# Masked softmax: batch 0 loaded as two contiguous megabytes from two queues

## The chip, the cores and the metric

One core of one Trainium2 chip. The metric is the device time of one execution in microseconds, as the median of several runs. A *span* is the length of the one execution that was profiled; it is some 1.6 us shorter than that execution's device time. A *packet* is one record of the trace's DMA table: one unbroken run of memory (8 or 16 KiB in most transfers) for SyncE and ScalarE, several short ones for GpSimd. The table doesn't name the DMA engine, so packets "per engine" are a count divided by 16.

## The reference

```python
batch, heads, seq_q, seq_k = 16, 8, 256, 256        # x: float32, 33.5 MB
for b in range(batch):
    length = lengths[b]                              # 128 <= length < 256
    masked = x[b, :, :, :length]
    masked = masked - np.max(masked, axis=-1, keepdims=True)
    e = np.exp(masked)
    result[b, :, :, :length] = e / np.sum(e, axis=-1, keepdims=True)   # the rest is 0
```

## The kernel before

A batch is 2048 rows of 256 columns, 2 MB. Partition p holds rows 16p to 16p + 15, which are 16 KiB in one piece of memory. There are eight slots of one batch each. SyncE issues the loads of batches 0 to 3 and all stores; GpSimd issues the loads of batches 4 to 15 and fetches only as many columns as the batch's length needs. VectorE clips the columns past the length to a huge negative number, ScalarE takes exponentials and row sums, and VectorE divides. A "half" is 8 of a partition's 16 rows.

```python
x_f   = x.rearrange("b h q k -> b (h q) k").rearrange("b (p t) k -> b p t k", p=P)
...
nc.scalar.dma_start(out=word64, in_=lengths[None, :]).then_inc(s_word, 16)
for h in range(2):                                   # batch 0 in two halves
    s = slice(h * half, (h + 1) * half)
    nc.sync.dma_start(out=xt[:, 0, s], in_=x_f[0, :, s]).then_inc(s_ld[h], 16)
for b in range(1, ahead):                            # batches 1, 2, 3 whole
    nc.sync.dma_start(out=xt[:, b], in_=x_f[b]).then_inc(s_ld[b + 1], 16)

nc.sync.wait_ge(s_exp, 3)                            # three half batches of exponentials
for b in range(batch):
    for s in parts(b):                               # batch 0 whole, later ones in halves or quarters
        nc.sync.wait_ge(s_out, 2 * b + (s.stop - 1) // half + 1)     # that part is divided
        ...
        nc.sync.dma_start(out=out_f[b, :, s, :], in_=xt[:, b % slots, s, :]).then_inc(...)
...
# GpSimd: waits for batch 2's landing, then two loads are under way at any time
nc.gpsimd.wait_ge(s_ld[ahead - 1], 16)
with nc.Fori(0, (batch - ahead) // 2, 1, engines=[POOL]) as q:
    for par in range(2):
        ...                                          # waits for load n-2 and store n-8
        pick(v_len, ...)                             # load of batch n, w of 256 columns
...
# VectorE's order
mask(0, slice(0, half)); mask(0, slice(half, nt))    # each waits for its half
for b in range(batch):
    ...                                              # divide(0, 0), mask(1), divide(0, 1), mask(2), ...
```

The softmax here doesn't subtract the row's maximum and nothing guards it: scores larger than these inputs give would overflow.

## Time and profile before

| | before |
|---|---|
| device time | 156.19 us, median of 3 (155.84 to 156.23) |
| moved | 62.08 MB at a mean of 401 GB/s |
| VectorE, ScalarE busy | 75%, 68% |
| clips of the two halves of batch 0 start | 6.60, 9.05 us |
| first store issued | 19.86 us |
| GpSimd's first load (batch 4) issued | 20.85 us |

The lines behind this table are shown in the prediction. The queues are named as the profile names them: q1 is SyncE's, q10 ScalarE's, q0 GpSimd's.

### The profile page before, as it was taken

Reading aid. Unit: us, or ns where it says so; the run is one execution under the profiler, and the core shown is the slowest. Engines: PE = TensorE matmul, PEld = TensorE weight load, DVE = VectorE, ACT = ScalarE, POOL = GpSimd, SP = SyncE. Lnnn points to the kernel's source line nnn. Section 1 sums busy time; section 2 is a strip of 40 time slices with the busy share of each in tenths; the row PEclk is TensorE's granted clock in tenths of the full one; section 3 lists DMA queues with packets and bytes.
Section 4 is the critical chain, followed back from the end, with each engine's and each line's share of the span. In section 5 each row is a group of like instructions: output and inputs, shape, how many; then the busy total and the mean of one; then the engine's idle time right before and its main releaser. Section 6 shows DMA issues by size and latency. Waiting matters only on the chain.

```text
span 154.7 us, 1324 instructions
## 1 busy us (share of the span) xinstructions
PE 0.2 (0%) x1; PEld 0.1 (0%) x1; DVE 115.7 (75%) x84; ACT 105.2 (68%) x514; POOL 19.0 (12%) x25
## 2 busy tenths in 40 slices
PE   0000000000000000000000000000000000000000
PEld 0000000000000000000000000000000000000000
DVE  1249999952999696979979696969689629796700
ACT  3087799992692959778695959595976906959200
POOL 4910031000220110201111020202001000000000
DMA  4999999999999999999999999999999999999992
GB/s 116 426 449 424 428 398 406 398 407 447 400 410 395 402 409 414 415 417 411 404 424 407 417 408 409 415 416 416 416 417 419 419 448 415 426 445 419 430 421 85
DMA packets 9988, 62.08 MB, mean 401 GB/s; under 512 B 850, under 2 KB 946, under 8 KB 6274
## 3 DMA queue, kind: packets, MB, share of 16 engines
q1 hardware_dynamic: 5904, 41.95, 65.8%
q0 software_dynamic: 4080, 20.12, 32.1%
q14 instruction: 2, 0.02, 0.0%
q10 hardware_dynamic: 2, 0.00, 0.0%
HBM read 28.51 MB, written 33.55 MB: 401 GB/s over the span
## 4 chain that ended last, share of the span: by engine, by line
DMA 55%; DVE 19%; ACT 8%; issue 8%; ACTq 2%; SPq 1%; POOLq 1%; DVEq 0%
DMA xt<-in_x_dram 34%; DMA out_dram<-xt 21%; DVE xt L222 9%; DVE xt L195 9%; ACT xt L252 8%; ACTq L252 2%; DVE inv_sum L219 1%; SPq L109 1%; POOLq L99 0%; SPq L111 0%; SPq L120 0%; DVEq L212 0%; POOLq L135 0%; POOLq L130 0%; ACTq L247 0%
## 5 line engine op out<-in xcount | busy, mean ns | idle before, releaser
L252 ACT ACTIVATE xt<-xt x256 | 102.4, 401 | 37.2 <-DVE xt L195 37.2
L222 DVE TENSOR_TENSOR xt<-xt,inv_sum 128x2048 f32<-128x2048 f32 x32 | 73.4, 2292 | 1.1
L252 ACT ACTIVATION_READ_ACCUMULATOR xt<-xt x256 | 47.9, 187 | 0.0
L195 DVE SCALAR_TENSOR_TENSOR xt<-down,len_s,xt 128x2048 f32<-128x2048 f32 (+1 forms) x17 | 37.8, 2222 | 13.1 <-DMA xt<-in_x_dram 13.0
L130 POOL DMA_DIRECT2D xt<-in_x_dram x12 | 12.8, 1064 | 95.5 <-issue 50.6
L219 DVE RECIPROCAL inv_sum<-row_sum 128x8 f32<-128x8 f32 x32 | 6.3, 198 | 14.4 <-ACT xt L252 14.4
L149 POOL MEMSET xt<- 128x1536 f32 x4 | 5.3, 1386 | 1.1 <-DVE len_s L186 1.1
L244 ACT ACT_TABLE_LOAD x1 | 1.3, 1283 | 1.6 <-SPq L81 1.6
L178 DVE TENSOR_SCALAR down<-iota_i 128x256 f32<-128x256 int32 x1 | 0.3, 297 | 1.6 <-POOL iota_i L141 1.6
L183 DVE CAST len_b<-word 1x16 bf16<-1x16 int32 x1 | 0.2, 163 | 0.4 <-DMA word<-in_lengths_dram 0.4
L186 DVE TENSOR_SCALAR len_s<-len_f 128x16 f32<-128x16 f32 x1 | 0.2, 174 | 0.3 <-PE len_f L165 0.3
L141 POOL IOTA iota_i<- 128x256 int32 x1 | 0.3, 331 | 0.6 <-SPq L81 0.6
L146 POOL MEMSET seed<- 1x1 f32 x2 | 0.3, 162 | 0.0
L244 ACT ACTIVATE warm<-const-float32-0.0 128x1 f32<-128x1 f32 x1 | 0.2, 203 | 0.0
L144 POOL MEMSET ones<- 1x128 bf16 x1 | 0.2, 194 | 0.0
L165 PE MATMUL len_f<-len_b,ones 1*128 1x16 bf16 x1 | 0.2, 164 | 2.6 <-DVE len_b L183 2.6
L275 POOL MEMSET const-float32-0.0<- 128x1 f32 x1 | 0.1, 98 | 0.3 <-issue 0.3
L165 PEld LDWEIGHTS len_f<-len_b,ones 1*128 1x128 bf16 x1 | 0.1, 99 | 2.6 <-POOL ones L144 2.6
L275 POOL MEMSET const-float32-1.0<- 128x1 f32 x1 | 0.1, 98 | 0.0
L275 POOL MEMSET const-bfloat16-1.0<- 128x1 bf16 x1 | 0.1, 98 | 0.0
L275 POOL MEMSET const-uint8-127<- 128x1 uint8 x1 | 0.1, 98 | 0.0
L275 POOL BASE_LOAD x1 | 0.0, 17 | 0.1
## 6 DMA issues: line engine op xcount, KB each, us to landing
out_dram<-xt SPq DMA_DIRECT2D x19, 1024.0 KB
out_dram<-xt SPq DMA_DIRECT2D x14, 512.0 KB
xt<-in_x_dram SPq DMA_DIRECT2D x3, 2048.0 KB, 16.1
out_dram<-xt SPq DMA_DIRECT2D x3, 2048.0 KB
xt<-in_x_dram POOLq DMA_DIRECT2D x3, 1728.0 KB, 16.9
xt<-in_x_dram POOLq DMA_DIRECT2D x2, 2048.0 KB, 18.5
xt<-in_x_dram POOLq DMA_DIRECT2D x2, 1600.0 KB, 16.8
xt<-in_x_dram POOLq DMA_DIRECT2D x2, 1280.0 KB, 14.8
```

Source lines behind the costliest of these rows:

```text
L109: nc.sync.dma_start(out=xt[:, 0, s], in_=x_f[0, :, s]).then_inc(s_ld[h], 16)
L130: nc.gpsimd.dma_start(out=xt[:, slot, :, :w], in_=x_n[:, n, :, :w]).then_inc(s_sw[par], 16)
L141: nc.gpsimd.iota(iota_i, pattern=[[1, seq_k]], base=0, channel_multiplier=0).then_inc(s_iota, 1)
L146: nc.gpsimd.memset(seed[:, par : par + 1], 0.0).then_inc(s_st[par], 64)
L149: nc.gpsimd.memset(xt[:, b, :, low:], 0.0).then_inc(s_fill, 1)
L165: nc.tensor.matmul(len_f, lhsT=ones, rhs=len_b, start=True, stop=True).then_inc(s_lenf, 1)
L195: return nc.vector.scalar_tensor_tensor(out=t, in0=down[:, None, lo:hi].to_broadcast([P, s.stop - s.start, hi - lo]), scalar=len_s[:, b : ...
L219: step(nc.vector.reciprocal(out=inv_sum[:, b, s], in_=row_sum[:, b, s]))
L222: nc.vector.tensor_tensor(out=t, in0=t, in1=inv_sum[:, b, s, None].to_broadcast([P, half, seq_k]), op=ALU.mult,).then_inc(s_out, 1)
L244: nc.scalar.activation(out=warm, in_=nc.const_aps.tensor(0.0, (P, 1), F32), func=EXP)
L252: ins = nc.scalar.activation(out=e, in_=e, func=EXP, accum_out=sum_h[:, bass.ds(i, 1), j])
L275: nc = _bacc.Bacc("TRN2", target_bir_lowering=False, num_devices=1)
```

## The change

Its intent is to get batch 0 in sooner: each half is one contiguous megabyte, and two queues issue the halves. As the rows of a partition change, the store of batch 0 changes with them, to two runs of 8 KiB per partition.

```diff
+    x_0 = x[0].rearrange("h q k -> (h q) k").rearrange("(u p t) k -> p u t k", u=2, p=P)
+    out_0 = out[0].rearrange("h q k -> (h q) k").rearrange("(u p t) k -> p u (t k)", u=2, p=P)
...
-        for h in range(2):
+        for h, queue in enumerate((nc.sync, nc.scalar)):
             s = slice(h * half, (h + 1) * half)
-            nc.sync.dma_start(out=xt[:, 0, s], in_=x_f[0, :, s]).then_inc(s_ld[h], 16)
+            queue.dma_start(out=xt[:, 0, s], in_=x_0[:, h]).then_inc(s_ld[h], 16)
...
-                nc.sync.dma_start(
-                    out=out_f[b, :, s, :], in_=xt[:, b % slots, s, :]
-                ).then_inc(s_b, 16 * ((s.stop - s.start) // quarter))
+                if b == 0:
+                    to = out_0
+                    at = xt[:, b, s, :].rearrange("p (u t) k -> p u (t k)", u=2)
+                else:
+                    to = out_f[b, :, s, :]
+                    at = xt[:, b % slots, s, :]
+                nc.sync.dma_start(out=to, in_=at).then_inc(s_b, 16 * ((s.stop - s.start) // quarter))
```

## The prediction

> **What bounds the kernel now.** I read the page first, for which resource is full.
>
> ```profile
> span 154.7 us, 1324 instructions
> PE 0.2 (0%) x1; PEld 0.1 (0%) x1; DVE 115.7 (75%) x84; ACT 105.2 (68%) x514; POOL 19.0 (12%) x25
> ...
> DMA  4999999999999999999999999999999999999992
> GB/s 116 426 449 424 428 398 406 398 407 447 400 410 395 402 409 414 415 417 411 404 424 407 417 408 409 415 416 416 416 417 419 419 448 415 426 445 419 430 421 85
> ...
> q1 hardware_dynamic: 5904, 41.95, 65.8%
> q0 software_dynamic: 4080, 20.12, 32.1%
> ```
>
> VectorE and ScalarE are idle a quarter and a third of the span. The DMA row is full in every slice but the first and the last. The 16 DMA engines move 62.08 MB at a mean of 401 GB/s, and that is the span: 62.08 / 401 = 154.8 us. So the kernel is bound by transfers. It can end earlier only if they start earlier, run at a higher rate, or lose less to holes; a later engine costs only what it turns into a hole. The measured time, 156.19, is 1.5 us above the span, and I keep that difference.
>
> Second, the start in order of time, since the change sits there. These lines are from the timeline (start, duration, idle time before and its cause).
>
> ```profile
> 1.09 0.52 ACTq L106 DMA_DIRECT2D word<-in_lengths_dram  x1
> 1.13 0.86 SPq L109 DMA_DIRECT2D xt<-in_x_dram  x2
> ...
> 2.05 1.91 SPq L111 DMA_DIRECT2D xt<-in_x_dram  x3
> ...
> 6.60 1.28 DVE L195 SCALAR_TENSOR_TENSOR xt<-down,len_s,xt 128x1024 f32<-128x1024 f32 x1 [3.61 <-DMA xt<-in_x_dram]
> 8.15 0.42 ACT L252 ACTIVATE xt<-xt  x1 [5.01 <-DVE xt L195]
> ...
> 9.05 1.29 DVE L195 SCALAR_TENSOR_TENSOR xt<-down,len_s,xt 128x1024 f32<-128x1024 f32 x1 [1.16 <-DMA xt<-in_x_dram]
> ...
> 16.54 0.42 ACT L252 ACTIVATE xt<-xt  x1 [1.90 <-DVE xt L195]
> ...
> 19.86 14.31 SPq L120 DMA_DIRECT2D out_dram<-xt  x7
> ...
> 20.85 1.29 POOL L130 DMA_DIRECT2D xt<-in_x_dram  x1 [12.46 <-issue]
> ```
>
> The reader is to see that the two halves of batch 0 land one after the other (VectorE's clips start at 6.60 and 9.05), and that SyncE's first store is issued at 19.86. The code lets that store go when ScalarE has finished its third half batch (the wait for three counts of exponentials). GpSimd issues the next load, of batch 4, at 20.85.
>
> Third, which queue carries the bytes after the first four loads. The DMA view of the window from 23 to 26 us shows:
>
> ```profile
> q1 hardware_dynamic: 77, 1.20, 97.8%
> q14 instruction: 1, 0.01, 0.6%
> ```
>
> GpSimd's queue, q0, has moved nothing yet, though its load was issued at 20.85; in the DMA view of 18 to 28 us it has moved just 0.09 MB. Between the end of the four first loads (about 22 us) and about 26 us, therefore, only SyncE's stores feed the DMA engines. This is the one place of the kernel where a delay of the compute can make a hole.
>
> Fourth, the rate by stage (the windows view; the last two numbers are the DMA share and GB/s).
>
> ```profile
> 2.00:4.00 2.00, 0.16 (x1) 0.10 (x1) 0.34 (x2) 1.13 (x2) 0.95 (x1) 1.00 0.88 250
> 4.00:8.00 4.00, 0.00 (x0) 0.00 (x0) 1.28 (x1) 0.00 (x0) 4.00 (x4) 1.00 1.04 436
> ...
> 16.00:20.00 4.00, 0.00 (x0) 0.00 (x0) 3.86 (x4) 3.46 (x17) 0.00 (x0) 1.00 1.00 426
> 20.00:22.00 2.00, 0.00 (x0) 0.00 (x0) 1.97 (x3) 2.00 (x11) 1.15 (x1) 1.00 1.08 418
> 22.00:24.00 2.00, 0.00 (x0) 0.00 (x0) 1.97 (x3) 2.00 (x11) 0.14 (x1) 1.00 0.92 360
> ```
>
> The half-megabyte pieces of batch 0 run at 436 GB/s from 4 to 8 us as they are, no slower than the whole 2 MB loads behind them (426). Only the first two microseconds are slow: 250 instead of about 430 GB/s costs 2 x (1 - 250/430) = 0.8 us.
>
> **What the Trainium skill says.** The page "DMA: Bandwidth & Descriptors", section "Issuing engines are not separate DMA queues", says that transfers issued by SyncE, ScalarE and GpSimd run on the same 16 engines and interleave, and that several issuers save only sequencer time. Its section "Queues, rings and completion order" says that each DMA engine goes round robin between the queues that have work, packet by packet. The trace agrees as far as it goes: later in the run q0 and q1 share a rate that stays at 400 to 420. The same page, "Latency and other measured facts", gives some 0.6 us to the first byte of a transfer issued by SyncE or ScalarE; here the first issue is at 1.13 and the first large packets show at about 2.1, so 1.0 us, and I use the trace. "HBM Reference", "Specifications", puts a core that streams alone at about 425 GB/s, limited by its DMA engines. The 426 between 16 and 20 us agrees: there is no higher rate for contiguous addresses to reach, apart from the slow first two microseconds.
>
> **The change part by part.**
>
> *Contiguous halves.* Which rows go to which partition changes, not the length of a run: 128 runs of 8 KiB per half, before and after. At 436 GB/s already, gain 0; on the slow start, between 0 and 0.3 us of the 0.8 (a guess). The store of batch 0 now writes two runs of 8 KiB per partition where there was one of 16 KiB. In the trace's packet records a packet of 8 KiB took about 0.309 us and one of 16 KiB 0.611, so 0.618 for two: over 2 MB (8 packets of 16 KiB per engine) 8 x 0.007 = 0.06 us.
>
> *Issue time.* SyncE's issue of the second half (0.42 us) goes, so batches 1 to 3 are issued 0.45 us earlier. They stand behind a full queue: gain 0. ScalarE pays about 0.45 us more before its table load and waits for data until 8.15 anyway: cost 0.
>
> *The first half lands later.* This is the step that matters. Before, the first half had the engines to itself, then the second. Now ScalarE's queue brings the second half about 0.5 us after the first (its issue follows the lengths, 1.09 + 0.52 = 1.61, against 1.13), and the engines alternate. Each half is 8 packets of 8 KiB per engine, 8 x 0.309 = 2.5 us alone, which is the gap of the two clips (9.05 - 6.60 = 2.45). The first half has had at most one packet per engine done when the second arrives; then it needs some 7 packets while 7 of the other half go between. It lands about 7 x 0.309 = 2.2 us later: first clip at about 8.7 instead of 6.60. The second half lands about where it did, 9.0 to 9.5.
>
> *What that delay does downstream.* First clip 8.7 to 10.0, second to 11.3, ScalarE starts at 8.7 + (8.15 - 6.60) = 10.25. Its two half batches of 3.2 us (8.15 to 11.35 before) run to 16.65. VectorE divides the first half at about 13.6 to 15.95, then clips batch 1, which had ended at 16.3 and now ends at about 18.4. So ScalarE starts batch 1 at 18.65 instead of 16.54, its third half batch ends at 21.9, and the first store is issued at 19.86 + 2.1 = 22.0.
>
> *What this does to the transfers.* The stores' first bytes follow 1.0 us after the issue: 23.0. The four loads, 8.39 MB at 425 GB/s = 19.7 us, plus 2.1 of start and about 0.6 net of slow start, end at about 22.4. q0 is silent till about 26. That is a hole of about 0.6 us (0.3 to 0.9), which adds whole, since the queues are full from there to the end and no stage later has spare rate. GpSimd's load of batch 4 waits for batch 2's landing at 18.60, unchanged because the bytes ahead of it are the same.
>
> *The later compute.* ScalarE runs without a pause from 16.54 to 35.8 and then VectorE sits idle for 4.4 us until batch 4 lands at 37.4. The 2 us delay disappears in that idle time: cost 0.
>
> Sum: + 0.6 (hole) + 0.06 (shorter runs of the store) - 0.15 (middle of the start's gain) = + 0.5 us on 156.19, so 156.7 us.
>
> **The rivals.** First: the halves do not alternate evenly, because SyncE's eight packets per engine are already taken when ScalarE's arrive, or the first half keeps priority. Then the first clip stays near 6.6 to 7.2, the store is issued near 20, no hole, and the time is 156.0 to 156.2. For it speaks the head start of 0.5 us; against it the round robin that the skill states. I give it 30%. Second: contiguous addresses, or two queues filling 16 idle engines, remove most of the slow start. That would give 0.5 us or so at the front: 155.7 with no hole, 156.2 with one. The slow packets are in the first two microseconds only while the same pitch later runs at full rate, which speaks against the addresses as the cause; 15%. Third: the delayed store sets back the slots that GpSimd reloads, so that loads stop later on. Loads of batches 8 and up wait for stores (GpSimd waits 44.9 us in all for them), so a delay of 2 us could show as more than one hole: 157.5 or more. Against it: the store queue only loses the 0.6 us of the hole, not the 2 us, and while one queue waits the other fills the engines (the DMA row is full all through); 10%. Fourth: the clip order. If the second half should land well before the first, nothing changes, as VectorE takes the halves in order.
>
> **Range and chances.** The parts span from 155.7 (start gained, no hole) to 157.3 (hole of 0.9 and a little given back later); the kernel before spreads 0.4 us over three runs. I take 156.7 with 155.7 to 157.5 for 8 in 10. Two per cent are 3.1 us: the front of the kernel before the first full slice holds only 0.8 us that could be gained, and to lose 3.1 us the whole 2.1 us delay and more would have to become a hole. Chances: faster 0.02, within 2% 0.95, slower 0.03.
>
> **What would show it right or wrong.** Right: q10 carries 1 MB; the first clip starts near 8.7 and the second follows at once; ScalarE's batch 1 starts near 18.6; the first store is issued near 22; the DMA share of 22 to 24 us falls below the 0.92 of before with a rate near 280 GB/s; the idle time of VectorE before batch 4's clip shrinks from 4.4 by about 2 us. If the first clip starts before 7.5, the alternation is wrong. If the first store is late and 22 to 24 us is as full as before, the hole is wrong, because GpSimd's queue or something else filled it. If 2 to 4 us runs well above 250 GB/s, the start was gained. If the time falls below 155.5, rates later in the run rose, for which I have no mechanism.

## The result, and the profile after

The changed kernel takes 156.97 us (156.83 to 157.33, 4 runs) against 156.16 (155.84 to 156.23, 4 runs). The ratio is 1.0059, with a 95% interval of 1.0037 to 1.0082: a small loss, clear of noise. Ratios here and below are the mean time of one kernel's fast runs over the mean of the other's fast runs of the same rounds, so they are not quite the ratio of the medians quoted beside them.

The kernel after still fills the DMA row, but two slices of its rate row (the sixth and seventh, about 19 to 27 us) are new:

```profile
span 155.7 us, 1324 instructions
...
DMA  4999989999999999999999999999999999999992
GB/s 122 436 457 408 438 324 298 420 431 416 404 394 420 409 417 410 417 411 405 427 406 411 410 406 419 402 416 419 420 419 438 421 429 425 425 452 425 417 425 101
```

In the kernel before these two slices read 398 and 406. The timeline of the kernel after says what came before it. Columns are start, duration, what ran, and in brackets the idle time ahead of it:

```profile
1.13 0.39 SPq L113 DMA_DIRECT2D xt<-in_x_dram  x1
...
1.66 0.38 ACTq L113 DMA_DIRECT2D xt<-in_x_dram  x1
...
6.17 1.28 DVE L203 SCALAR_TENSOR_TENSOR xt<-down,len_s,xt 128x1024 f32<-128x1024 f32 x1 [3.15 <-DMA xt<-in_x_dram]
...
13.73 1.28 DVE L203 SCALAR_TENSOR_TENSOR xt<-down,len_s,xt 128x1024 f32<-128x1024 f32 x1 [6.28 <-DMA xt<-in_x_dram]
...
20.43 1.29 POOL L138 DMA_DIRECT2D xt<-in_x_dram  x1 [12.02 <-issue]
...
23.29 17.20 SPq L130 DMA_DIRECT2D out_dram<-xt  x7
```

The first half is not later, as predicted, but 0.43 us earlier (6.17 against 6.60). The second half, though it was issued at 1.66, is clipped at 13.73 instead of 9.05, 4.7 us later. VectorE and ScalarE take the halves in order, so the first store is issued 3.4 us later. The DMA view of the kernel after, first from 2.2 to 5.2 us and then from 6 to 12, shows how it came so late:

```profile
q1 hardware_dynamic: 120, 0.98, 91.0%
```

```profile
q1 hardware_dynamic: 112, 1.84, 71.3%
q10 hardware_dynamic: 103, 0.84, 33.2%
```

Columns are packets, MB and the share of the 16 engines. In the first window ScalarE's queue moves nothing at all: by the packet records its first packet comes at 5.7 us, when the whole first half and one packet per engine of batch 1 have been started. In the second the queues take turns, almost one packet for one (112 and 103). But SyncE is by then on batch 1, whose packets are 16 KiB each, while the second half's are 8 KiB: it gets a third of the rate.

The same happens again at the stores. From 23 to 26 us the kernel before had only SyncE's stores on the engines; the kernel after has only GpSimd's load of batch 4:

```profile
q0 software_dynamic: 187, 0.90, 92.9%
```

That is 0.90 MB in 3 us where the kernel before moved 1.20. By the trace's packet records GpSimd's load enters at 22.5 us (before: 26.5), and the stores, issued at 23.29, have their first packet at 27.2.

The account in bytes comes from the windows view; its last two columns are the DMA share and GB/s. The kernel before:

```profile
4.00:22.00 18.00, 0.00 (x0) 0.00 (x0) 12.88 (x10) 11.96 (x59) 5.54 (x5) 1.00 1.02 430
22.00:28.00 6.00, 0.00 (x0) 0.00 (x0) 5.97 (x4) 6.00 (x31) 0.70 (x2) 1.00 0.95 380
28.00:60.00 32.00, 0.00 (x0) 0.00 (x0) 26.16 (x20) 22.61 (x113) 3.45 (x3) 1.00 1.02 412
60.00:150.00 90.00, 0.00 (x0) 0.00 (x0) 70.01 (x50) 63.13 (x312) 7.47 (x7) 1.00 1.02 419
```

The kernel after:

```profile
2.00:4.00 2.00, 0.17 (x1) 0.10 (x1) 0.34 (x2) 1.49 (x2) 0.92 (x1) 1.00 0.96 274
4.00:22.00 18.00, 0.00 (x0) 0.00 (x0) 9.48 (x7) 8.64 (x43) 5.71 (x5) 1.00 1.02 436
22.00:28.00 6.00, 0.00 (x0) 0.00 (x0) 5.93 (x6) 6.00 (x32) 0.56 (x1) 1.00 0.86 256
28.00:60.00 32.00, 0.00 (x0) 0.00 (x0) 29.68 (x21) 27.20 (x136) 4.61 (x4) 1.00 1.02 415
60.00:150.00 90.00, 0.00 (x0) 0.00 (x0) 69.46 (x49) 61.87 (x306) 6.31 (x6) 1.00 1.02 419
```

Rate times length gives megabytes. Up to 22 us the kernel after is ahead by 2 x 24 + 18 x 6 = 0.16 MB. Between 22 and 28 us it loses 6 x 124 = 0.74 MB. Until 60 it makes good 32 x 3 = 0.10. From there both run at 419. Net 0.48 MB behind, which at 419 GB/s is 1.1 us; the spans differ by 1.0. So the whole loss of the kernel is made between 22 and 28 us. Half of it, 2 x (360 - 170) = 0.38 MB, falls in the first two of these six microseconds, when the engines were busy for only 60% of the time (before: 92%):

```profile
22.00:24.00 2.00, 0.00 (x0) 0.00 (x0) 2.00 (x2) 2.00 (x12) 0.56 (x1) 1.00 0.60 170
```

From 24 to 28 us they were busy (1.02 and 0.97), but carried 310 and 289 GB/s where the kernel before carried 414 and 365.

### The profile page after: what moved, and what is told of

Its sections match the earlier page's. It is cut to its first block, busy times and chain, and to the rows that moved or that the text cites. A ratio compares the mean times of both kernels' runs of the same rounds, so it can differ in the third digit from the quotient of the medians.

```text
span 155.7 us, 1324 instructions
## 1 busy us (share of the span) xinstructions
PE 0.2 (0%) x1; PEld 0.1 (0%) x1; DVE 115.2 (74%) x84; ACT 105.2 (68%) x514; POOL 19.0 (12%) x25
## 4 chain that ended last, share of the span: by engine, by line
DVE 38%; issue 24%; ACT 15%; DMA 8%; ACTq 5%; DVEq 1%; SPq 0%
DVE xt L203 23%; ACT xt L260 15%; DVE xt L230 12%; DMA xt<-in_x_dram 8%; ACTq L260 4%; DVE inv_sum L227 2%; DVEq L220 1%; ACTq L110 0%; ACTq L255 0%; ACTq L294 0%; SPq L85 0%
```

## The experiments

Twelve kernels ran; all gave the right result. "First clip", "second clip" and "first store" are starts in each run's timeline. A profile is one execution, and those of two kernels with the same time differed by 0.16 MB (0.4 us) in such an account (the kernel before, and the first experiment's, which carried 346 GB/s from 22 to 28 us instead of 380).

**1. Which part: addresses or queue?** The contiguous halves with both issued by SyncE:

```diff
-        for h, queue in enumerate((nc.sync, nc.scalar)):
+        for h, queue in enumerate((nc.sync, nc.sync)):
```

> The contiguous halves alone, both issued by SyncE. Theory (the queue costs, the layout doesn't): second clip near 8.9 us as in the kernel before, first store issued near 19.6, no hole between 22 and 24 us, time 155.7 to 156.2 (the front a little faster: 0.0 to 0.4 us). Rival (the layout costs, through the 8 KiB runs of batch 0's store or of its address pattern): 156.7 to 157.2 even so.

156.16 us, ratio 0.9989 (0.9966 to 1.0012). First clip 6.32, second 8.75, first store 19.58. The layout alone costs nothing that five rounds can see. It starts the first clip 0.3 us earlier, and the end doesn't move.

And the old addresses, with the second half on ScalarE's queue:

```diff
-        for h in range(2):
-            nc.sync.dma_start(out=xt[:, 0, s], in_=x_f[0, :, s])...
+        for h, queue in enumerate((nc.sync, nc.scalar)):
+            queue.dma_start(out=xt[:, 0, s], in_=x_f[0, :, s])...
```

> The kernel before with its second half issued by ScalarE, addresses as before. Theory (the queue costs): second clip near 13.7 us, first store issued near 23.3, a rate under 200 GB/s between 22 and 24 us, time 156.9 to 157.3. Rival (it takes both parts, or the layout costs): under 156.5.

157.71 us, ratio 1.0092 (1.0071 to 1.0113), more than expected. First clip 6.60, second 14.13, first store 23.69. The second queue alone gives the loss. It is larger than that of the whole change (1.0059); the intervals overlap, so whether contiguous addresses give some of it back isn't settled.

**2. Is it the late store?** The loads stay untouched, and the first store of the kernel before is held longer:

```diff
-        nc.sync.wait_ge(s_exp, 3)
+        nc.sync.wait_ge(s_exp, 4)
```

> The kernel before, but the first store waits for four half batches of exponentials instead of three, so that it is issued near 23.0 instead of 19.86; loads and queues untouched. Theory (the late first store is what costs): GpSimd's queue gets in first, at about 22.4 us instead of 26.4, the stores' first packet comes near 27, 22 to 28 us carries some 0.5 to 0.7 MB less than in the kernel before, time 156.8 to 157.2. Rival (the late second half costs in another way, for instance by the compute of batches 0 to 3): 156.1 to 156.4.

157.59 us, ratio 1.0092 (1.0070 to 1.0114), again more than expected. The clips are those of before (6.61, 9.06), the store is issued at 23.08, GpSimd's first packet comes at 22.9 and the stores' at 26.9. The window from 22 to 28 us of this run:

```profile
22.00:28.00 6.00, 0.00 (x0) 0.00 (x0) 5.97 (x4) 6.00 (x31) 0.72 (x2) 1.00 0.86 252
```

Nearly the rate of the kernel after the change (256), with nothing done to the loads: 6 x (380 - 252) = 0.77 MB lost. A late first store is enough for all of the loss. The rival, that the late second half costs by way of the compute, isn't needed.

**3. Why does ScalarE's half wait?** Its half is issued ahead of the lengths, within 0.04 us of SyncE's (1.09 and 1.13):

```diff
-        nc.scalar.dma_start(out=word64, in_=lengths[None, :]).then_inc(s_word, 16)
         for h, queue in enumerate((nc.sync, nc.scalar)):
             ...
+        nc.scalar.dma_start(out=word64, in_=lengths[None, :]).then_inc(s_word, 16)
```

> The changed kernel, but ScalarE issues the second half ahead of the lengths, at 1.1 instead of 1.66 us, so that both halves reach the engines together. Theory (the queue that comes second waits behind what the engines already hold of the first; two that come together alternate): q10 starts near 2.2 instead of 5.5 us, first clip 8.2 to 9.0, second clip 8.9 to 10.2, first store issued near 22, a hole of about half the size, 156.4 to 156.9. Rival (SyncE's queue goes first whenever it has a transfer of its own): q10 starts at 5.2 to 5.6 again, first clip near 6.2, second near 13.7, 156.9 to 157.3.

157.24 us, ratio 1.0063 (1.0043 to 1.0082). The queues share at once: in the DMA view from 3.5 to 7 us of this run

```profile
q10 hardware_dynamic: 90, 0.74, 49.7%
q1 hardware_dynamic: 87, 0.71, 48.4%
```

By the packet records SyncE's queue starts 0.85 us after ScalarE's, when the first packet of each engine is through. But the run is a bad test of the time: the lengths now stood behind the half in ScalarE's queue and were used only at 8.90 us, so the first clip started at 10.45 and the store at 23.70. The expected 22 was missed for that reason.

To have both, SyncE issued an unused copy of the lengths first, so that the halves went out at 1.52 and 1.65 us with the lengths early:

```diff
+        nc.sync.dma_start(out=spare, in_=lengths[None, :]).then_inc(s_spare, 16)
...                                                      # and SyncE waits for it ahead of its first store
+        nc.sync.wait_ge(s_spare, 16)
```

> The changed kernel, with a second, unused copy of the lengths issued by SyncE ahead of the first half, so that both halves are issued near 1.66 us and the lengths are early. Theory (two that arrive together alternate at once; 0.5 us of lead is what kept ScalarE's queue out): q10 starts by 3.2 us, first clip 8.6 to 9.6, second within 1.3 us of the first, first store issued at 21.8 to 22.8: the course that the prediction described. Time 156.6 to 157.3. Rival (SyncE's queue always goes first): q10 starts after 5 us, first clip near 6.7, second near 14.

157.41 us, ratio 1.0085 (1.0069 to 1.0102). First clip 8.26, second 11.04, first store 21.57. With a lead of 0.13 us ScalarE's queue entered at 4.4 us, later than expected; from then on the share was even. The second clip came 2.8 us after the first, not within 1.3, and the time is just above the range. Only part of this run's loss lies between 22 and 28 us (351 GB/s); 168 GB/s from 2 to 4 us and 405 from 28 to 60 make up most of the rest. In these three runs the second queue's delay grows with its lag. Counting the first queue's large packets that had started before the second queue's first one gives, per engine, 1.0 with a lag of 0.04 us, 3.8 with 0.13 us, and 9.0 in the changed kernel with 0.53 us, where a half is 8 packets per engine.

**4. What is it that the engines hold?** The first half as two quarters in 4 KiB runs:

```diff
-            queue.dma_start(out=xt[:, 0, s], in_=x_0[:, h]).then_inc(s_ld[h], 16)
+            for g in range(2 if h == 0 else 1):          # SyncE's half in two transfers
+                n = quarter if h == 0 else half
+                queue.dma_start(out=xt[:, 0, s.start + g * n : s.start + (g + 1) * n],
+                                in_=x_0[:, h, g * n : (g + 1) * n]).then_inc(s_ld[h], 16)
...                                                      # and VectorE waits for both quarters
```

> The changed kernel, with the first half issued by SyncE as two quarters of 4 KiB runs. What the engines hold before the other queue gets in: if it is one transfer, ScalarE's queue starts near 3.9 us and the first clip is late (7 to 8.5), the second earlier than 13.7; if it is a number of bytes or a time, it starts near 5.6 us as before, first clip near 6.2 to 6.6, second near 13.7, time 156.8 to 157.3; if it is a number of packets (8 per engine), near 3.9 as well, but with the second quarter alternating.

157.82 us, ratio 1.0121 (1.0104 to 1.0139). ScalarE's queue entered at 4.6 us, after 8.3 packets per engine but only 33 KB, against 9.0 packets and 80 KB. It isn't an amount of bytes. These runs can't tell a transfer from some eight packets, as each of SyncE's transfers is eight packets per engine. The stores that wait behind GpSimd's load fit neither. In six of the runs with a late store (the kernel after among them) their first packet came 3.8 to 4.0 us after their issue. Meanwhile GpSimd's queue started 11.6 to 14.9 packets of 4.8 KB per engine, out of 21 in that load, or, in experiment 8, 5.4 packets of 16 KiB. There the time is steadier than any count, and no experiment varies it. What a late queue waits for stays open; that it waits is shown. First clip 9.14, later than any of the forecasts; second 11.07, first store 22.39.

**5. Turns by packet or by share?** Batch 1 in two halves of 8 KiB runs, everything else as after the change:

```diff
-            nc.sync.dma_start(out=xt[:, b], in_=x_f[b]).then_inc(s_ld[b + 1], 16)
+            for g in range(2 if b == 1 else 1):
+                s = slice(g * half, (g + 1) * half) if b == 1 else slice(0, nt)
+                nc.sync.dma_start(out=xt[:, b, s], in_=x_f[b, :, s]).then_inc(s_ld[b + 1], 16)
...                                                      # and VectorE waits for both halves of batch 1
```

> The changed kernel, with batch 1 loaded in two halves of 8 KiB runs instead of whole in 16 KiB runs. Theory (once in, the two queues take turns packet by packet, so the second half gets 8 of every 24 KiB beside 16 KiB packets and 8 of 16 beside 8 KiB packets): second clip at 11.0 to 11.6 instead of 13.73, first store issued near 21, time between 156.2 and 156.8. Rival (ScalarE's queue gets a fixed third, or its own packets are slow): second clip stays near 13.7 and the time near 156.9.

The mechanism is as expected: second clip 11.41, first store 20.98, and from 6 to 10 us the queues share evenly:

```profile
q1 hardware_dynamic: 109, 0.87, 51.2%
q10 hardware_dynamic: 104, 0.85, 50.2%
```

The turn is one packet, be it of 8 or of 16 KiB. The time was a miss: 157.00 us, ratio 1.0058 (1.0044 to 1.0073), no better than the changed kernel, though 22 to 28 us is nearly whole at 357 GB/s: this run falls behind after 28 us instead (see 6). The control has the same split of batch 1, with both halves of batch 0 on SyncE (the edit above on the kernel of the first experiment):

> Contiguous halves and all loads on SyncE, with batch 1 in two halves of 8 KiB runs: the control for the run that had the second half on ScalarE's queue and batch 1 split (157.0). If the split itself costs: 156.6 to 157.0. If not (theory): 155.8 to 156.3, and that run's loss comes from its later second half and store.

156.55 us, ratio 1.0025 (1.0006 to 1.0044), above what was expected. The split itself seems to cost some 0.3%. If that adds to the rest, the earlier second half brought part of the loss back; but the two runs come from different rounds on different chips, and the part is no larger than their intervals, so it isn't shown.

**6. A store a little late.** The kernel before, with its first store held until batch 2 is clipped:

```diff
-        nc.sync.wait_ge(s_exp, 3)
+        nc.sync.wait_ge(s_min, 6)
```

> The kernel before, with its first store held until batch 2 is clipped: issued near 21.2 us, between the 19.86 of before and the 23.08 of the run that was held for four half batches. Its first bytes then come at about 22.2, when the four loads end, so there is no gap on SyncE's queue. Theory (the loss is the time in which the engines have nothing but GpSimd's load): 156.0 to 156.4. Rival (it is enough that GpSimd's load enters ahead of the stores, gap or not): GpSimd's first packet near 23 instead of 26.4, time 156.7 to 157.2, which would also explain the run with batch 1 in two halves.

156.63 us, ratio 1.0036 (1.0018 to 1.0054); store issued at 21.09. Neither expectation holds. SyncE's queue has no gap and GpSimd's first packet comes at 25.8, so there was nothing to lose in the first theory's terms, and yet some 0.6 us are lost. GpSimd's load was issued at 20.73, ahead of the store, and still entered 3.4 us after it: the order of issue alone doesn't say which queue goes first, and here SyncE's queue was still at work on its loads. The windows place most of the loss after 28 us: 403 instead of 412 GB/s from 28 to 60, which the runs with batch 1 in two halves and with two copies of the lengths show too (404 and 405). What slows those 32 us is open. So a late store can cost without a hole, too.

**7. Is the store only a microsecond too late?** The changed kernel without the long wait:

```diff
-        nc.sync.wait_ge(s_exp, 3)
+        nc.sync.wait_ge(s_exp, 1)
```

> The changed kernel without the wait that holds the first store for three half batches of exponentials: it then goes when batch 0 is divided, near 22.2 us instead of 23.29. Theory (a queue that comes second, here the stores behind GpSimd's load, waits until the engines are through with what they hold of the first): the stores' first packet still comes at 26.5 to 27.5 us, the time stays at 156.7 to 157.2. Rival (the stores are only a microsecond too late and enter as soon as they are issued): first packet at 23.2, no hole after it, 156.0 to 156.5.

157.05 us, ratio 1.0066 (1.0054 to 1.0078). The store is issued at 22.39, 0.9 us earlier, and its first packet comes at 26.3, just ahead of the range; no gain shows in the time. From 23 to 26 us GpSimd's load is alone again, with 0.76 MB. SyncE's queue, too, waits when it comes second.

**8. Why is GpSimd's load slow when alone?** Batch 4 fetched whole, in runs of 16 KiB instead of 800 B (200 columns):

```diff
-        with nc.Fori(0, (batch - ahead) // 2, 1, engines=[POOL]) as q:
+        nc.gpsimd.dma_start(out=xt[:, ahead], in_=x_f[ahead]).then_inc(s_sw[0], 16)
+        ...                                              # batch 5 as before
+        with nc.Fori(1, (batch - ahead) // 2, 1, engines=[POOL]) as q:
```

> The changed kernel, with batch 4 loaded whole (16 KiB runs, 2048 KB) instead of 200 of its 256 columns (800 B runs, 1600 KB). Theory (between 24 and 27 us GpSimd's queue has the engines alone, and its short runs are what makes them slow there): 24 to 26 us carries 390 GB/s or more instead of 314, the 0.46 MB more to load cost about what the higher rate brings, 156.4 to 157.4. Rival (GpSimd's queue alone is slow whatever its runs): 24 to 26 us stays under 330 GB/s and the time rises to 157.8 to 158.4.

157.24 us, ratio 1.0074 (1.0061 to 1.0088), for 0.46 MB more to move. From 23 to 26 us of this run:

```profile
q0 software_dynamic: 74, 1.21, 104.5%
```

1.21 MB where the short runs moved 0.90 (24 to 26 us: 401 GB/s against 310), and the engines were busy in both (104.5% and 92.9%). So GpSimd's queue isn't slow alone whatever its runs. How short runs slow it is open: the median packet of the short runs (six runs, 4800 B, in 188 ns) kept the pace of a 16 KiB packet (612 ns), and it is a minority of them that took much longer. From 24 to 27 us the rates are 355 and 288 GB/s, and the reason why both fall off there is open too. The load was also issued 1.3 us sooner, because the first round of the loop was unrolled; that helps at 22 us. Over 22 to 28 us this run carries 373 GB/s, close to the 380 of the kernel before: the hole is all but gone, and what is left of the loss (0.74%, 1.2 us) is what 0.46 MB more take at 419 GB/s (1.1 us).

**9. Would an earlier store gain?** Contiguous halves on SyncE, and the store freed at once, the candidate for a version that beats both:

```diff
-        nc.sync.wait_ge(s_exp, 3)       # on the kernel of the first experiment
+        nc.sync.wait_ge(s_exp, 1)
```

> Contiguous halves, all on SyncE, without the wait for three half batches: the first store is issued when batch 0 is divided, near 18.4 us. Theory (the stores already stand behind the loads in the queue at 19.6, an earlier issue brings nothing): 155.8 to 156.4. Rival (an earlier store gains as a later one loses): under 155.7, which would beat both kernels.

156.18 us, ratio 1.0006 (0.9990 to 1.0023), with the store issued at 18.54. It brings nothing: no run here beats the kernel before.

## Why the prediction was right or wrong

- **Time and direction: right.** 156.97 measured, 156.7 predicted, inside 155.7 to 157.5, and within 2%. The main reason given, that a later first store leaves the DMA engines short after 22 us, is what the run with only a held store shows.
- **Bound: right.** Both spans are bytes over rate, and the loss is entirely a shortfall in bytes.
- **Alternation of the halves: wrong.** This is the step that failed: "the engines alternate" from about 0.5 us on, so that the first clip starts at 8.7 and the second at 9.0 to 9.5. Measured: 6.17 and 13.73. The first rival (the first half keeps the engines) was right about the first clip, but concluded no late store and no loss. It missed that the second half then has to share with batch 1's packets of twice its size. The step let the turn-taking start when the second transfer arrives, some 0.5 us after the first; here it started 3.6 us after the first queue's first packet, 9.0 packets per engine on.
- **First store: right in kind, too small.** 22.0 predicted, 23.29 measured, since the delay came by way of the second half (4.7 us) instead of the first (2.1 us). "The stores' first bytes follow 1.0 us after the issue" was wrong as well: they came 3.9 us after it.
- **"q0 is silent till about 26": wrong.** GpSimd's queue was silent in the kernel before because SyncE's queue went on without a gap, not because it was slow. With a gap there it entered at 22.5. From 24 us on the hole was thus filled, but with 800 B runs at about 300 GB/s, and the stores were in turn kept out till 27.2.
- **Size of the hole: mis-sized.** Predicted 0.6 us, with 22 to 24 us near 280 GB/s. Measured 170 GB/s there, and 0.74 MB lost from 22 to 28 us, 1.8 us at 419 GB/s. What brought the sum back near the prediction are two terms that were too small or absent: 0.16 MB gained by 22 us (0.4 us, against 0.15) and 0.10 MB made good after 28 us (0.2 us, against none). The first may belong to this one profile: experiments 7 and 8, whose first loads are the same, had gained only 0.03 and 0.04 MB by 22 us. The sum was nearly right by errors that cancelled, which is luck.
- **Issue time, store runs, later compute: no cost, right as far as shown.** The layout with both halves on SyncE measured 0.9989. VectorE's idle 4.4 us before batch 4's clip took up the delay: after the change that clip starts at 36.35 us without a wait (before: 37.62). The rival of more holes later is not seen in the kernel after (415 and 419 GB/s after 28 us).
- **Readings to correct.** The halves of batch 0 are one megabyte each, not "half-megabyte pieces". The rate that the two queues share later on reads 395 to 448 in the slices, not 400 to 420, and a shared rate says nothing of turns. The same trace has 436 and 438 GB/s, so 425 is not the highest rate to be had.

## What to carry to other kernels

In this kernel, whose transfers never stop, a second queue added no bandwidth (430 and 436 GB/s from 4 to 22 us); it changed who goes first. So follow the transfer that the compute order needs next, and ask what it will stand behind. A queue that falls half a microsecond behind may wait for several, as here (3.6 us), and then shares by packet, so that its share depends on the other queue's packet size. When a queue is silent in a profile, ask whether it is slow or only kept out before building on its silence.

## What the Trainium skill lacked or had wrong

- "DMA: Bandwidth & Descriptors", "Queues, rings and completion order", has each DMA engine go round robin between its queues packet by packet, with some 9 to 17 descriptors to a packet. Once both are in, the runs agree on the turns: 112 packets against 103, and 109 against 104. But the turns were of a single run of 8 or 16 KiB: ScalarE's eight packets per engine, 2.5 us if taken in one go, were spread from 5.7 to 12.5 us. What the page lacks is the entry: a queue that lagged by 0.04, 0.13 and 0.53 us got in only after 1.0, 3.8 and 9.0 packets per engine of the other's.
- The same page, "Issuing engines are not separate DMA queues", says that a second issuer only saves issue time. It also changes the order in which data lands: the second half was clipped at 13.73 instead of 9.05 us, and the kernel lost 0.6%.
- The same page, "Specifications", puts full line rate at runs of 512 B and more. That isn't the whole of it: GpSimd's load in 800 B runs, nearly alone on busy engines, moved 0.90 MB in 3 us (299 GB/s); in 16 KiB runs 1.21 MB (404 GB/s). The median packet does keep the pace (4800 B in 188 ns, 16 KiB in 612 ns), so the loss lies in the slower packets, and why they are slow is open.
- The same page, "Latency and other measured facts", gives about 0.6 us to the first byte of a transfer from SyncE or ScalarE, and the section doesn't say from when. Here it was 1.0 us from the start of SyncE's issue (1.13 to 2.15), but 0.6 from its end (1.52), which agrees. No run here shows GpSimd's queue start on free engines.
